# Convolution taps at fixed, spread places in VectorE's order; its mixing, the gate's stores and a weight split moved

## The chip, the cores and the metric

The kernel runs on one core of one Trainium2 chip. The metric is the device time of one execution in microseconds, the median of several runs. A profiled execution of the same kernel gives the trace.

## The reference

One layer over a sequence of 2048 tokens of 1024 features (float32). The input is normalised, projected once, and mixed in three ways: chunked attention (6 heads), a convolution of 31 taps over 256 channels, and retention (6 heads). The three outputs go through one output projection onto the residual; then come a feed-forward part and a gated embedding. What the change touches is the convolution and the gate at the end:

```python
def conformer_conv(u, conv_w, conv_b, ln_g, ln_b, pw_w, pw_b):
    a, gate = jnp.split(u, 2, axis=-1)
    glu = a * jax.nn.sigmoid(gate)
    y = lax.conv_general_dilated(glu, conv_w[:, None, :], window_strides=(1,),
        padding=[(CONV_K - 1, 0)], feature_group_count=D_CONV, ...)
    y = layernorm(y + conv_b, ln_g, ln_b)
    y = jax.nn.silu(y)
    return y @ pw_w + pw_b

h = h + jnp.concatenate([att, conv, ret], axis=-1) @ w_o[i]
h = h + jnp.square(jax.nn.relu(rmsnorm(h, norm_ffn_g[i]) @ w1[i])) @ w2[i]
gate = jax.nn.sigmoid(rmsnorm(h, norm_ple_g[i]) @ w_pg[i])
h = h + gate * (p[i] @ w_ple[i])
```

## The kernel before

The sequence is worked through in four blocks of 512 tokens (b = 0 to 3). Features lie on partitions, tokens along the free dimension. Each product is made of three matmuls, since every operand is split into a high and a low part (names ending in h and l, or two slices of a weight tile w); the low part of a weight is a subtraction `wsplit` (L125 to L127) on VectorE or GpSimd, after ScalarE has made the high part. A weight is loaded raw and split at its first use, stored to DRAM split (`wstage`, L129), and afterwards loaded split (`wunit`, L133, load at L139). Weight tiles have five buffers, raw loads two.

The stages of a block are: the convolution's projection (four chunks, `conv_proj`, L293); in blocks 1 to 3 then the gate of the block before (two halves of four columns, `gate`, L746); three pairs of an attention projection ap and a retention projection rp; the output projection (two parts); eight feed-forward groups. The gate of block 3 comes at the very end. For a column j of the gate TensorE makes 24 matmuls into a bank acc and 6 into a bank ple. VectorE reads acc (L768), ScalarE takes the sigmoid, VectorE multiplies with ple (L771), POOL adds to h (L772), and SP stores h to `out` (L773). Accumulators acc have two banks.

TensorE's instructions are pinned to their written order (`tc.keep_in_program_order`, L48 to L59): an instruction so pinned comes right behind the instruction of its engine that was written before it. All others are placed by a scheduler that goes by readiness and priority: `tc.high_priority(offset=...)` moves a priority, and LATE is the lowest one. Side work is woven into the written order by position: `place` names points along TensorE's work where the next step of a generator is written, `spread` gives evenly spaced points, and `chain` paces a generator between a start and an end point (L808 to L846). So attention's mixing (`att_mix`) is written among the matmuls of ap and rp: its scores are sc on TensorE, the biased scores with their row extreme pt on VectorE (L472), their transposes back in sc, copied to pT on VectorE (L486), and their product with v in po.

The convolution itself has two groups of 128 channels, and for each a first tap L338 and 30 more L340, all on VectorE with 128x512 elements: y = gl * weight + y. Before, the 62 taps of a block are written at the end of `conv_proj` at priority LATE. `conv_mix` (L352) takes y: transposes on TensorE to the bank cvt, a layer norm on VectorE and POOL (z), transposes back to the bank cvb, silu and split on ScalarE and VectorE, and the pointwise product into the bank cpw.

Of the kernel before, what the change touches and what calls it, by code (L numbers as in the profile page):

```python
# [14 lines left out]
ALU = mybir.AluOpType  # L15
AX = mybir.AxisListType

P = 128
D = 1024
S = 2048  # L20
T = 512
NB = S // T
# [5 lines left out]
NTAP = 31  # L28
# [6 lines left out]
LATE = -1000  # L35
# [5 lines left out]
def trunk(ctx, tc, a, out):  # L41
    nc = tc.nc
    V, A, G = nc.vector, nc.scalar, nc.gpsimd
# [29 lines left out]
    def stile(tag, bufs, shape, name=None, dt=F32):  # L73
        return sp.tile(list(shape), dt, tag=tag, name=name or tag, bufs=bufs)
# [16 lines left out]
    def tmp(name, n):  # L91
        return stile("t", 4, [P, n], name)
# [4 lines left out]
    def cv(name, dt=F32, n=T):  # L97
        return stile("cv", 5, [P, n], name, dt)
# [19 lines left out]
    def f(t):  # L118
        return t.bitcast(F32)


    def wtile():
        return stile("w", 5, [P, 2, 2, HALF], "w", F32R)

    def wsplit(w, x, n, eng):  # L125
        A.activation(w[:, 0, :n], x, AF.Copy)  # L126
        eng.tensor_tensor(w[:, 1, :n], x, f(w[:, 0, :n]), ALU.subtract)  # L127
# [5 lines left out]
    def wunit(name, i, n=HALF):  # L133
        key = name + "_".join(map(str, i))
        seen[key] = seen.get(key, 0) + 1
        with tc.high_priority(offset=AHEAD):
            u = wtile()
            if key in kept:
                nc.sync.dma_start(f(u)[:, :, :, :n], kept[key])  # L139
            else:  # L140
                raw = rawt("raw")
                nc.sync.dma_start(raw[:, : 2 * n], a[name][i])
                for c in range(2):
                    wsplit(u[:, c], raw[:, c * n : c * n + n], n, (G, V)[c])
        if key not in kept and seen[key] == (2 if name == "w2" else 1):
            wstage(key, u, n)
        return [u[:, 0], u[:, 1]]
# [11 lines left out]
    def cost(n):  # L159
        return 3 * n / 2400.0  # L160

    def stream(name, *i):
        got = {}

        def blk(n):
            if n // 8 not in got:
                got.clear()
                got[n // 8] = wunit(name, (*i, n // 8))
            return tuple(got[n // 8][n % 8 // 4][:, s, (n % 4) * P : (n % 4) * P + P] for s in range(2))

        return blk
# [88 lines left out]
    cur = {}  # L260
# [32 lines left out]
    def conv_proj(blk):  # L293
        xh, xl = cur["x"]
        hi, lo = (lambda k: xh[:, k]), (lambda k: xl[:, k])
        gls = []

        def sigmoid(b):
            sig = tmp("sig", T)
            V.tensor_tensor(sig, b, cur["R"], ALU.mult)  # L300
            A.activation(sig, sig, AF.Sigmoid)
            G.tensor_tensor(sig, sig, cur["R"], ALU.mult)
            return sig

        def glu(c, b, sig):
            gl = cv("gl", n=T + NTAP - 1)
            V.tensor_copy(gl[:, : NTAP - 1], hist[:, c])
            V.tensor_tensor(gl[:, NTAP - 1 :], b, sig, ALU.mult)
            V.tensor_copy(hist[:, c], gl[:, T:])
            gls.append(gl)  # L310

        if blk == 0:
            ss = [sb2("cvp") for _ in range(2)]
            bs = [s[:, i * 512 : i * 512 + 512] for s in ss for i in range(2)]
            for i in range(4):
                if i == 3:
                    cur["R"] = cv("R")
                    bcast(cur["r"], cur["R"])
                yield from stat_steps(cur["w"][i], KT, hi, lo, bs[i], T)
            for c in range(2):  # L320
                glu(c, bs[2 * c + 1], sigmoid(bs[2 * c]))
        else:
            for c in range(2):
                if c == 0:
                    cur["R"] = cv("R")
                    bcast(cur["r"], cur["R"])
                b = accb()
                yield from stat_steps(wstat("wc", 2 * c), KT, hi, lo, b, T)
                sig = sigmoid(b)
                b = accb()  # L330
                yield from stat_steps(wstat("wc", 2 * c + 1), KT, hi, lo, b, T)
                glu(c, b, sig)
        ys = []
        with tc.high_priority(offset=LATE):
            for c in range(2):
                gl = gls[c]
                y = cv("y")
                V.tensor_scalar(y, gl[:, :T], cw[:, c, 0:1], cvec[:, 0, c : c + 1], ALU.mult, ALU.add)  # L338
                for j in range(1, NTAP):
                    V.scalar_tensor_tensor(y, gl[:, j : j + T], cw[:, c, j : j + 1], y, ALU.mult, ALU.add)  # L340
                ys.append(y)
        cur["ys"] = ys

    def load_pw():
        cur["pw"] = pww = ctile("pww", [P, 2, 2 * DC], dt=F32R)
# [400 lines left out]
    def gate(blk, half):  # L746
        xh, xl = cur["x3"]
        h = cur["h"]
        tk = slice(blk * T, blk * T + T)
        pt = cur["pt"]  # L750
        w = stream("w_g", half)
        for i in range(4):
            j = 4 * half + i
            end = blk == NB - 1 and j == KT - 1
            ws = [w(10 * i + k) for k in range(10)]
            for x in (slice(0, T // 2), slice(T // 2, T)) if end else (slice(0, T),):
                n = x.stop - x.start
                gt = tmp("gate", T)[:, :n]
                o = None
                for k in (*range(2), *range(2, 10)) if j == 0 else (*range(2, 10), *range(2)):  # L760
                    if k == 0:
                        o = e = sb2("ple")[:, :n]
                    elif k == 2:
                        o = b = accb()[:, :n]
                    y = pt[k] if k < 2 else (xh[:, k - 2], xl[:, k - 2])
                    yield from mm3s(o, ws[k], (y[0][:, x], y[1][:, x]), k in (0, 2), k in (1, 9))
                    if k == 9:
                        V.tensor_tensor(gt, b, cur["r3"][:, x], ALU.mult)  # L768
                        A.activation(gt, gt, AF.Sigmoid)
                    if k == (9 if j == 0 else 1):  # L770
                        V.tensor_tensor(gt, gt, e, ALU.mult)  # L771
                        (V if end else G).tensor_tensor(h[j][:, x], h[j][:, x], gt, ALU.add)  # L772
                        nc.sync.dma_start(out[j * P : j * P + P, blk * T + x.start : blk * T + x.stop], h[j][:, x])  # L773
                    yield cost(n) / 3

    kvc = [(None, None)] * NPAIR
    ng_ = DFF // 512
# [28 lines left out]
    AS, RS, RT0, CS, CE, RE, LE, LF, NE, NF, GE, GF, AS0, CS0, CE0 = 0.25, 0.35, 0.03, 0.4, 0.5, 0.95, 0.4, 0.7, 0.4, 0.55, 0.16, 0.22, 0.25, 0.5, 0.5  # L806

    def at(name, frac):  # L808
        s, c = start[name]
        return s + frac * c  # L810

    def spread(n, t0, t1):
        return [t0 + (t1 - t0) * i / (n - 1) for i in range(n)]

    def place(gen, ts):
        tasks.append([ts, gen, None])
# [3 lines left out]
    def chain(i, gen, start, end):  # L820
        chains[i].append([start, end, gen, None, 0.0])

    L = NB - 1
    place(load_pw, [at(("ap", 0, 0), 0.5)])
    for b in range(NB):
        if b:
            place(lambda b=b: xnorm(b), spread(13, at(("g2", b - 1, 6), 0.05), at(("g2", b - 1, 7), 0.95)))
            place(late, spread(8, at(("conv", b), 0.01), at(("conv", b), LE)))
            place(lambda b=b: ple_load(b - 1), [at(("conv", b), 0.3)])
            place(late_rstd, [at(("conv", b), LF), at(("conv", b), LF + 0.28)])  # L830
        if b:
            chain(1, conv_mix, at(("ap", b, 0), CS), at(("ap", b, 1), CE))
        for p in range(NPAIR):
            nxt = ("rp", b, p + 1) if p < 2 else ("wob", b)
            chain(0, lambda p=p: att_mix(p), at(("rp", b, p), AS if b or p else AS0), at(nxt, AS if p < 2 else 0.0))
            chain(1, lambda p=p: ret_mix(p), at(("ap", b, p + 1), RS) if p < 2 else at(("woa", b), RT0),
                  at(nxt, RE if p < 2 else 0.0))
            if b == 0 and p == 0:
                chain(1, conv_mix, at(("ap", b, 1), CS0), at(("rp", b, 2), CE0))
        place(norm2, [at(("g1", b, 0), NE), at(("g1", b, 0), NF)])  # L840
    place(lambda: ple_load(L), [at(("g2", L, 7), 0.0)])
    place(late_rstd, [at(("gate", L, 0), GE), at(("gate", L, 0), GF)])

# [35 lines left out]
    raw = rawt("raw")  # L879
    u = wtile()  # L880
    with tc.high_priority(offset=3 * AHEAD):
        nc.sync.dma_start(ng, a["norm_g"])
    for c in range(2):
        with tc.high_priority(offset=AHEAD):
            next(first)
        x = slice(c * HALF, c * HALF + HALF)
# [16 lines left out]
    cw = ctile("cw", [P, 2, NTAP], a["conv_w"])  # L903
    cvec = ctile("cvec", [P, 4, 2], a["cvec"])
# [114 lines left out]
```

## Time and profile before

| | us |
|---|---|
| median of 3 runs (lowest, highest) | 2763.8 (2763.01, 2765.96) |
| the profiled execution | 2768.22 |
| its span, first to last instruction | 2766.4 |
| TensorE busy in it | 2683.5 (97%) |
| VectorE busy | 1344.3 (49%) |
| ScalarE busy | 745.3 (27%) |
| GpSimd busy | 717.6 (26%) |

The mean granted clock of TensorE over the span is 0.99 of full speed. The names of the engines in rows are PE (TensorE; PEld its weight loads), DVE (VectorE), ACT (ScalarE), POOL (GpSimd) and SP (SyncE, which issues the DMAs; SPq is its sequencer). A busy share is an average over stages of different limits: of TensorE's idle time, what counts is which wait ended last, and on what.

### The profile page before, as it was taken

The numbers are of one execution on the slowest core, as the hardware profiler recorded it, in microseconds if no ns is written. First come the engines' busy times: TensorE is split into PE (matmuls) and PEld (weight loads), VectorE is DVE, ScalarE is ACT, GpSimd is POOL, SyncE is SP. The second block draws the span as 40 slices with busy tenths as digits, with TensorE's granted clock in tenths as the row PEclk, the third lists the DMA queues.
The fourth block names the chain that finished last, engine by engine and source line by source line (L and its number), as shares of the span: only waits on it lengthen the run. The fifth ranks groups of instructions, "written<-read, shape, count | busy, mean of one in ns | idle before, by whom it ended". The sixth has DMA issues, their size and how long they took to land.

```text
span 2766.4 us, 34253 instructions
## 1 busy us (share of the span) xinstructions
PE 2683.5 (97%) x13178; PEld 2236.1 (81%) x13178; DVE 1344.3 (49%) x2297; ACT 745.3 (27%) x1506; POOL 717.6 (26%) x676
## 2 busy tenths in 40 slices
PE   7899999999899999999999999999999999999999
PEld 6777788887788888888888888888887888888887
DVE  5966655457745543334664554222376555322222
ACT  4454322234144321112324432000122442100011
POOL 4334534334312231222322213001022221210112
PEclk9999999999999999999999999999999999999999
DMA  7647664656633566767663345555655344555554
GB/s 270 237 146 259 230 215 170 208 176 219 206 121 128 193 212 231 259 222 261 240 208 116 132 156 210 187 194 195 231 191 178 117 151 160 190 192 189 197 195 147
DMA packets 123281, 535.35 MB, mean 194 GB/s; under 512 B 12784, under 2 KB 38128, under 8 KB 77040
## 3 DMA queue, kind: packets, MB, share of 16 engines
q1 hardware_dynamic: 123120, 533.17, 54.7%
q8 instruction: 104, 1.70, 0.3%
q14 instruction: 57, 0.47, 0.1%
HBM read 412.54 MB, written 120.59 MB: 193 GB/s over the span
## 4 chain that ended last, share of the span: by engine, by line
PE 82%; DVE 8%; DMA 4%; ACT 2%; issue 2%; POOL 1%; SPq 0%; DVEq 0%; ACTq 0%; POOLq 0%
PE acc L54 46%; PE w L54 26%; DVE y L340 4%; PE po L54 2%; PE sc L54 2%; PE sc L59 2%; DMA w<-k_wr 1%; PE rout L54 1%; DVE w L127 1%; PE ple L54 1%; PE rsc L54 1%; DMA w<-k_wa 1%; DVE k L445 1%; ACT q L447 0%; DMA raw<-in_wc_dram 0%
## 5 line engine op out<-in xcount | busy, mean ns | idle before, releaser
L54 PE MATMUL acc<-xh,w 128*128 128x512 f32 (+1 forms) x1744 | 549.1, 391 | 8.3 <-DVE gate L768 4.0
L54 PE MATMUL acc<-w,xh 128*128 128x512 f32 (+1 forms) x1536 | 469.0, 380 | 18.0 <-DMA w<-k_wa 6.7
L54 PEld LDWEIGHTS acc<-xh,w 128*128 128x128 f32 x1744 | 327.0, 188 | 80.0 <-issue 5.2
L54 PE MATMUL acc<-hid,w 128*128 128x512 f32 x1536 | 367.0, 392 | 0.0
L54 PE MATMUL w<-hid,w 128*128 128x512 f32 x1536 | 362.0, 391 | 0.0
L54 PEld LDWEIGHTS acc<-hid,w 128*128 128x128 f32 x1536 | 288.4, 188 | 63.6
L54 PEld LDWEIGHTS w<-hid,w 128*128 128x128 f32 x1536 | 288.5, 188 | 63.1
L54 PEld LDWEIGHTS acc<-w,xh 128*128 128x128 f32 x1536 | 287.8, 194 | 61.1 <-DMA w<-k_wr 9.5
L54 PE MATMUL acc<-xl,w 128*128 128x512 f32 (+1 forms) x872 | 335.0, 389 | 0.9 <-DVE xl L234 0.9
L54 PE MATMUL w<-xh,w 128*128 128x512 f32 x1024 | 322.0, 390 | 0.0
L127 POOL TENSOR_TENSOR w<-raw,w 128x512 fp32r<-128x512 f32 (+1 forms) x141 | 186.7, 1325 | 506.3 <-ACT w L126 486.6
L692 POOL TENSOR_TENSOR s<-r 128x512 f32<-128x512 f32 x128 | 157.7, 1233 | 554.9 <-DVE r L691 554.9
L126 ACT ACTIVATE w<-raw 128x512 fp32r<-128x512 f32 (+1 forms) x284 | 160.9, 614 | 498.1 <-PE acc L54 279.6
L54 PE MATMUL acc<-w,xl 128*128 128x384 f32 (+1 forms) x768 | 289.2, 377 | 0.0
L693 ACT ACTIVATE hid<-r 128x512 fp32r<-128x512 f32 x128 | 80.2, 628 | 576.3 <-DVE r L691 576.3
L54 PEld LDWEIGHTS w<-xh,w 128*128 128x128 f32 x1024 | 191.9, 188 | 39.7
L127 DVE TENSOR_TENSOR w<-raw,w 128x512 fp32r<-128x512 f32 (+1 forms) x143 | 180.5, 1263 | 81.9 <-ACT w L126 76.7
L340 DVE SCALAR_TENSOR_TENSOR y<-gl,cw,y 128x512 f32<-128x512 f32 x240 | 207.4, 893 | 2.5
L54 PE MATMUL w<-xl,w 128*128 128x512 f32 x512 | 199.2, 389 | 0.0
L54 PEld LDWEIGHTS acc<-xl,w 128*128 128x128 f32 x872 | 164.2, 188 | 36.1 <-DVE xl L234 1.3
L718 DVE TENSOR_TENSOR h<-h,w 128x512 f32<-128x512 f32 x128 | 87.9, 688 | 197.4 <-PE w L54 196.6
L718 DVE TENSOR_TENSOR h<-h,acc 128x512 f32<-128x512 f32 x128 | 87.8, 687 | 173.3 <-PE acc L54 172.8
(182 smaller groups left out, 3291.2 us busy)
## 6 DMA issues: line engine op xcount, KB each, us to landing
w<-k_w SPq DMA_DIRECT2D x160, 1024.0 KB, 4.8
k_w<-w SPq DMA_DIRECT2D x64, 1024.0 KB, 6.8
raw<-in_w_dram SPq DMA_DIRECT2D x96, 512.0 KB, 4.5
w<-k_wr SPq DMA_DIRECT2D x36, 1024.0 KB, 5.9
w<-k_w_g SPq DMA_DIRECT2D x30, 1024.0 KB, 4.8
w<-k_wa SPq DMA_DIRECT2D x36, 768.0 KB, 6.0
w<-k_w_oa SPq DMA_DIRECT2D x18, 1024.0 KB, 6.1
k_wr<-w SPq DMA_DIRECT2D x12, 1024.0 KB, 7.0
```

Of the source, the lines that this page charges most:

```text
L54: tc.keep_in_program_order(nc.tensor.matmul(o, x, y, start=start, stop=stop))
L59: tc.keep_in_program_order(nc.tensor.transpose(o, x, i))
L126: A.activation(w[:, 0, :n], x, AF.Copy)
L127: eng.tensor_tensor(w[:, 1, :n], x, f(w[:, 0, :n]), ALU.subtract)
L340: V.scalar_tensor_tensor(y, gl[:, j : j + T], cw[:, c, j : j + 1], y, ALU.mult, ALU.add)
L445: V.scalar_tensor_tensor(lo, bj, gain[x, 0:1], f(hi), ALU.mult, ALU.subtract)
L692: G.tensor_tensor(s, r, r, ALU.mult)
L693: A.activation(hid[:, j], r, AF.Square)
L718: V.tensor_tensor(h[j], h[j], b, ALU.add)
```

## The change

It has four parts.

- The taps leave `conv_proj` and become a generator `taps`. Each tap is pinned in VectorE's order behind the instruction written before it, and the 62 are written at evenly spaced points: in block 0 from 0.05 of ap of the first pair to 0.45 of ap of the second; in blocks 1 to 3 from 0.02 of the gate's first half to 0.8 of ap of the first pair.
- In blocks 1 to 3 `conv_mix` is written from 0.9 of the first ap to 0.95 of the first rp, instead of from 0.4 of the first ap to 0.5 of the second ap.
- In `gate` a store is held and issued at k == 6 of the next column, pinned in SP's order; the last of a half is issued at its end.
- The gate's weights w_g are split on GpSimd in both halves (before: one half on GpSimd, one on VectorE). They are split in block 1 only, 10 units, so 10 instructions of 128x512 change engine.

```diff
-                    wsplit(u[:, c], raw[:, c * n : c * n + n], n, (G, V)[c])
+                    wsplit(u[:, c], raw[:, c * n : c * n + n], n, G if name == "w_g" else (G, V)[c])
...
-        ys = []
-        with tc.high_priority(offset=LATE):
-            for c in range(2):
-                gl = gls[c]
-                y = cv("y")
-                V.tensor_scalar(y, gl[:, :T], cw[:, c, 0:1], cvec[:, 0, c : c + 1], ALU.mult, ALU.add)
-                for j in range(1, NTAP):
-                    V.scalar_tensor_tensor(y, gl[:, j : j + T], cw[:, c, j : j + 1], y, ALU.mult, ALU.add)
-                ys.append(y)
-        cur["ys"] = ys
+        cur["gls"] = gls
+
+    def taps():
+        ys = cur["ys"] = []
+        for c in range(2):
+            gl = cur["gls"][c]
+            y = cv("y")
+            ys.append(y)
+            for j in range(NTAP):
+                x, g = gl[:, j : j + T], cw[:, c, j : j + 1]
+                if j == 0:
+                    i = V.tensor_scalar(y, x, g, cvec[:, 0, c : c + 1], ALU.mult, ALU.add)
+                else:
+                    i = V.scalar_tensor_tensor(y, x, g, y, ALU.mult, ALU.add)
+                tc.keep_in_program_order(i)
+                yield
...
-                        nc.sync.dma_start(out[j * P : j * P + P, blk * T + x.start : blk * T + x.stop], h[j][:, x])
+                        held.append((out[j * P : j * P + P, blk * T + x.start : blk * T + x.stop], h[j][:, x]))
+                    if held and (end or k == 6):
+                        tc.keep_in_program_order(nc.sync.dma_start(*held.pop()))
                     yield cost(n) / 3
+
+        while held:
+            tc.keep_in_program_order(nc.sync.dma_start(*held.pop()))
...
+    for b in range(NB):
+        if b:
+            place(taps, spread(2 * NTAP, at(("gate", b - 1, 0), 0.02), at(("ap", b, 0), 0.8)))
+        else:
+            place(taps, spread(2 * NTAP, at(("ap", 0, 0), 0.05), at(("ap", 0, 1), 0.45)))
...
-            chain(1, conv_mix, at(("ap", b, 0), CS), at(("ap", b, 1), CE))
+            chain(1, conv_mix, at(("ap", b, 0), 0.9), at(("rp", b, 0), 0.95))
```

What the change moves in the order of the engines is shown at three places. "xN" means that a row stands N times in a row; lines are those of the version itself (in the changed one the taps are L344 and L346).

The first is VectorE in block 0, from the keys k of the first pair of heads to the score reductions (ISA pt,nm) of its first tile. Before:

```order
L445 SCALAR_TENSOR_TENSOR k<-qkT,kg,k 64x512
L566 RECIPROCAL e<-e 128x128
L445 SCALAR_TENSOR_TENSOR k<-qkT,kg,k 64x512
L472 ISA pt,nm<-sc,bias 128x128
L472 ISA nm 128x1
L340 SCALAR_TENSOR_TENSOR y<-gl,cw,y 128x512
L472 ISA pt,nm<-sc,bias 128x128
L472 ISA nm 128x1
```

And in the changed kernel, from the first reduction on:

```order
L478 ISA pt,nm<-sc,bias 128x128
L478 ISA nm 128x1
L346 SCALAR_TENSOR_TENSOR y<-gl,cw,y 128x512
L451 SCALAR_TENSOR_TENSOR k<-qkT,kg,k 64x512
L346 SCALAR_TENSOR_TENSOR y<-gl,cw,y 128x512
L571 TENSOR_SCALAR e<-e 128x128
L346 SCALAR_TENSOR_TENSOR y<-gl,cw,y 128x512
L572 RECIPROCAL e<-e 128x128
L346 SCALAR_TENSOR_TENSOR y<-gl,cw,y 128x512
L344 TENSOR_SCALAR y<-gl,cw,cvec 128x512
L346 SCALAR_TENSOR_TENSOR y<-gl,cw,y 128x512 x13
L478 ISA pt,nm<-sc,bias 128x128
```

Between the second k and the second reduction stand 17 taps, where none stood between the two and one between the reductions. Ahead of the second k stand 13 taps, where 28 stood.

The second is VectorE in block 1, around the gate's first columns (gate<-acc, L768 and in the changed kernel L775). Before, behind the second gl:

```order
L308 TENSOR_TENSOR gl<-acc,sig 128x512
L340 SCALAR_TENSOR_TENSOR y<-gl,cw,y 128x512
L127 TENSOR_TENSOR w<-raw,w 128x512
L309 COPY hist<-gl 128x30
L340 SCALAR_TENSOR_TENSOR y<-gl,cw,y 128x512
L338 TENSOR_SCALAR y<-gl,cw,cvec 128x512
L340 SCALAR_TENSOR_TENSOR y<-gl,cw,y 128x512 x5
L127 TENSOR_TENSOR w<-raw,w 128x512
L768 TENSOR_TENSOR gate<-acc,r_5326 128x512
L340 SCALAR_TENSOR_TENSOR y<-gl,cw,y 128x512 x2
L771 TENSOR_TENSOR gate<-gate,ple 128x512
L340 SCALAR_TENSOR_TENSOR y<-gl,cw,y 128x512 x4
```

In the changed kernel, behind the second gl as well:

```order
L308 TENSOR_TENSOR gl<-acc,sig 128x512
L309 COPY hist<-gl 128x30
L344 TENSOR_SCALAR y<-gl,cw,cvec 128x512
L346 SCALAR_TENSOR_TENSOR y<-gl,cw,y 128x512 x5
L775 TENSOR_TENSOR gate<-acc,r_5326 128x512
L778 TENSOR_TENSOR gate<-gate,ple 128x512
L346 SCALAR_TENSOR_TENSOR y<-gl,cw,y 128x512 x5
L775 TENSOR_TENSOR gate<-acc,r_5326 128x512
L346 SCALAR_TENSOR_TENSOR y<-gl,cw,y 128x512
L778 TENSOR_TENSOR gate<-gate,ple 128x512
```

The taps of the first channel group no longer stand ahead of the second gl, and the splits w are gone from VectorE. So it goes on, with six taps or so to each column; 13 taps are left behind the last column.

The third is SP in block 1: the last stores of the gate (out_dram) and the loads of the attention weights (w<-k_wa) among them. Before:

```order
L139 DMA w<-k_wa_0_414 128x4x384
L773 DMA out_dram<-h 128x512
L131 DMA k_w_g_4_5798<-w 128x2048
L139 DMA w<-k_wa_1_423 128x4x384
L773 DMA out_dram<-h 128x512
L139 DMA w<-k_wa_2_432 128x4x384
L773 DMA out_dram<-h 128x512
L139 DMA w<-k_wa_3_441 128x4x384
```

In the changed kernel:

```order
L139 DMA w<-k_wa_0_350 128x4x384
L782 DMA out_dram<-h 128x512
L131 DMA k_w_g_4_5778<-w 128x2048
L139 DMA w<-k_wa_1_359 128x4x384
L782 DMA out_dram<-h 128x512
L139 DMA w<-k_wa_2_368 128x4x384
L782 DMA out_dram<-h 128x512
L139 DMA w<-k_wa_3_377 128x4x384
```

The rows are the same; in both, four stores stand ahead of the first of these loads.

## Rows read from the trace of the kernel before

**Rows 1.** The page: busy time by engine, the chain by engine, the taps' group.

```profile
PE 2683.5 (97%) x13178; PEld 2236.1 (81%) x13178; DVE 1344.3 (49%) x2297; ACT 745.3 (27%) x1506; POOL 717.6 (26%) x676
...
PE 82%; DVE 8%; DMA 4%; ACT 2%; issue 2%; POOL 1%; SPq 0%; DVEq 0%; ACTq 0%; POOLq 0%
...
L340 DVE SCALAR_TENSOR_TENSOR y<-gl,cw,y 128x512 f32<-128x512 f32 x240 | 207.4, 893 | 2.5
```

**Rows 2.** TensorE's waits: us in total, times, longest us.

```profile
PE sc L54 <- DVE k L445: 21.6, 22, 2.6
PE qkT L59 <- POOL an L416: 10.2, 4, 6.6
...
PE acc L54 <- DMA w<-k_wa: 6.7, 3, 5.3
...
PE acc L54 <- DVE gate L768: 4.2, 4, 1.6
...
PE acc L54 <- DVE gl L308: 2.3, 1, 2.3
```

**Rows 3.** Windows: length, busy PE, PEld, DVE, ACT, POOL (count), clock, DMA.

```profile
80.00:120.00 40.00, 37.15 (x205) 31.96 (x206) 37.71 (x81) 17.54 (x52) 12.97 (x14) 0.94 0.62 226
...
695.00:735.00 40.00, 35.99 (x154) 28.54 (x154) 39.56 (x48) 6.30 (x11) 14.48 (x10) 1.00 0.72 251
```

**Rows 4.** VectorE's timeline in block 0: start us, us, instruction, idle before.

```profile
79.15 0.75 DVE L445 SCALAR_TENSOR_TENSOR k<-qkT,kg,k 64x512 fp32r<-64x512 f32 x1
...
80.81 0.28 DVE L472 CUSTOM_DVE_ANT_0 pt<-sc,bias 128x128 f32<-128x128 f32 x1
...
134.48 4.97 DVE L340 SCALAR_TENSOR_TENSOR y<-gl,cw,y 128x512 f32<-128x512 f32 x5
```

**Rows 5.** Timelines of VectorE and POOL: taps beside POOL's splits, taps alone.

```profile
58.38 2.77 DVE L340 SCALAR_TENSOR_TENSOR y<-gl,cw,y 128x512 f32<-128x512 f32 x2
...
58.90 3.39 POOL L127 TENSOR_TENSOR w<-raw,w 128x512 fp32r<-128x512 f32 x2
...
686.74 3.38 DVE L340 SCALAR_TENSOR_TENSOR y<-gl,cw,y 128x512 f32<-128x512 f32 x5
```

**Rows 6.** TensorE's timeline in block 0, scores and keys.

```profile
87.09 0.38 PE L59 MATMUL sc<-ident,pt 128*128 128x128 f32 x2
...
94.87 0.66 PE L59 MATMUL sc<-ident,pt 128*128 128x128 f32 x4
...
99.40 0.44 PE L54 MATMUL sc<-k,q 128*128 128x384 f32 x1 [1.44 <-DVE pT L486]
...
141.06 1.33 PE L59 MATMUL qkT<-ident,an 128*128 128x128 f32 x5 [6.59 <-POOL an L416]
...
154.63 0.63 PE L59 MATMUL cvt<-ident,y 128*128 128x128 f32 x4 [2.35 <-DVE z L371]
```

**Rows 7.** TensorE's timeline in block 1; the last row is of the chain.

```profile
681.76 0.39 PE L54 MATMUL acc<-xh,w 128*128 128x512 f32 x1
...
739.58 0.62 PE L54 MATMUL acc<-w,xh 128*128 128x384 f32 x2 [0.17 <-DVE gate L768]
...
748.78 1.01 PE L54 MATMUL acc<-w,xh 128*128 128x384 f32 x2 [5.28 <-DMA w<-k_wa]
...
1010.20 10.88 PE acc L54 x48
```

**Rows 8.** Timelines of VectorE, POOL and SP: column 6 of the gate.

```profile
738.85 0.68 DVE L768 TENSOR_TENSOR gate<-acc,r 128x512 f32<-128x512 f32 x1
...
740.99 1.30 POOL L772 TENSOR_TENSOR h<-h,gate 128x512 f32<-128x512 f32 x1 [5.77 <-DVE gate L771]
...
742.78 0.53 SPq L139 DMA_DIRECT2D w<-k_wa  x1
```

**Rows 9.** Timelines of VectorE and TensorE in block 2, last gate and transposes.

```profile
1423.55 0.69 DVE L771 TENSOR_TENSOR gate<-gate,ple 128x512 f32<-128x512 f32 x1 [0.71 <-ACT gate L769]
...
1431.09 0.60 PE L59 MATMUL cvt<-ident,y 128*128 128x128 f32 x4
```

More of the change, by code (lines that the diff above doesn't have):

```diff
@@ L751, in gate @@
         w = stream("w_g", half)
+        held = []
         for i in range(4):
```

## Prediction

> **What bounds the kernel now.** I read the page's busy shares and chain first, then TensorE's waits, the windows, and at the end the timelines of the two stretches where the change moves rows. TensorE is busy 2683.5 us of the 2766.4 us span, and by the chain 82% of the span is TensorE's and 8% VectorE's [rows 1]. So all that can be won is TensorE's idle time of some 83 us and the slow clock behind each stall, and only where a stall stands. The waits show which ones end on VectorE or on something behind it [rows 2]: sc on k 21.6 us, qkT on POOL's an 10.2, acc on the gate 4.2, acc on gl 2.3, and acc on the load of k_wa 6.7. The feed-forward stretches have none of these and no tap, so they stay as they are. The windows [rows 3] show where VectorE is short: busy 37.71 of 40 us in block 0's scores, and 39.56 in the gate that block 1 does for block 0.
>
> **Block 0: taps in a worse place.** Before, a tap was VectorE's last choice and filled idle time: 28 of 62 taps stood ahead of the second k (L445) [rows 4]. Now each tap is pinned behind its neighbour. The order has 13 ahead of that k, and 17 between it and the second score reduction, where one stood. A tap alone takes 0.67 us (3.38 for five) [rows 5]. The 15 that no longer fill the wait for weights and keys cost 15 x 0.67 = 10.0 us later, in the stretch with 37.71 of 40 us taken.
> Going down the new order by the old durations: the second k ends near 78.1 (79.90 before; it waits for fewer taps). Then 17 x 0.67 = 11.4, and 1.1 for an e and a reciprocal: the reduction, at 80.81 before [rows 4], starts near 90.6. TensorE's transposes of the first tile's pt, at 87.09 before [rows 6], start near 91.3 (+4). From 91.0, ten taps (6.7) and 2.6 us of rotary rows and a split lead to the copy pT at 100.3. Six more taps and the same other rows lead to the second tile's reductions near 108, its transposes near 110.4 (94.87 before, +15.5) and the third tile's second scores near 117.3 (99.40 before, +17.9).
> By then nearly all taps are done, while before 17 were still to come: 17 x 0.67 = 11.4 us lighter. That is where TensorE waited 6.59 us for qkT and 2.35 for cvt [rows 6]. I take these two, 8.9 us, as won back: **+9**. Bounds: +6.5 if the whole 11.4 come back, +17.9 if nothing does. I take a value near the low end, because right before the longer of these waits ended VectorE had five taps in a row, 4.97 us [rows 4].
>
> **Block 1: gates less late.** After the last product of the first gate bank (681.76) seven more banks of 30 matmuls at 0.227 us (10.88 for 48) [rows 7] take 47.6 us, so attention could start near 729.7. It started at 739.58, after 2.3 us of waits on gl, 4.2 on gates [rows 2] and slower matmuls behind them. Then came 5.28 us for k_wa [rows 7]: SP issued this load at 742.78, behind the store of column 6 of the gate, which waits for POOL's add at 740.99, and this for VectorE's gate row at 738.85 [rows 8]. So what counts is when VectorE reaches column 6.
> In the new order both gl stand ahead of all taps, 42 taps stand ahead of this gate row where 62 did, and the ten splits of w_g are POOL's. The first tap can start near 676 (second gl, whose bank TensorE finishes a little before). 42 x 0.667 = 28.0, and six pairs of gate rows at 1.3 make 7.8. POOL's work takes time from VectorE: two taps beside two of POOL's splits took 2.77 us instead of 1.4 [rows 5], and the mean tap is 893 ns [rows 1]. I take 1.05 us for each POOL instruction of 128x512 that falls on a tap; twelve splits and six adds do: 18.9. Sum 730.7 against 738.85: **-8.1**, and k_wa lands as much earlier. The ends of that price: at nothing VectorE reaches column 6 at 711.8, ahead of TensorE (724.3), the load is issued near 728 and lands near 734, where it is wanted at 733.6: -14.7. At 1.44 us a piece the gate comes at 737.7: -1. By the same sum the banks of columns 4 to 6 are read 6 to 8 us late, just inside the 8.2 us (36 matmuls) that two banks allow.
> The rows show that a tap beside POOL is stretched by about its own length. The Trainium skill, in "SBUF — State Buffer", section "Who interferes with whom", is stricter: a VectorE instruction with two inputs in SBUF and a GpSimd instruction that reads SBUF share a port pair, which the first one holds for its whole instruction while the other is blocked. By that rule a tap may wait POOL's whole 1.30 us [rows 8], 23.4 us for the 18, and block 1 would gain 3.6 only. The trace shows less, some 1.05, and the sum goes by that.
>
> **Later stores.** A store is held until k = 6 of the next column, but on SP each load of k_wa keeps the number of stores ahead of it: four, five, six and seven. The last still stands right behind the store of column 6. I cost this at 0: SP, the only queue these are on, waits at that place for POOL in any case. POOL's add of column 3 now stands behind five splits and may be some 5 us later; nothing in VectorE's order waits for it before column 7.
>
> **The mixing later, blocks 1 to 3.** The same matmuls, transposes and ScalarE rows, moved. The transposes of y stand 48 matmuls of 128x384 further on (8.3 us at 0.173), and cvb follows qkT at once, so that silu and yh stand on ScalarE between the rows that make k. In blocks 2 and 3 the waits for k_wa (6.7 in three, of which 5.28 are block 1's) may go, while sc's waits on k grow by 0.3 to 0.5: -0.5 a block, **-1** together. Thirteen taps now stand between the last gate row and the transposes. From 1424.2 [rows 9] they (8.7), two pairs of ass rows and the waits for these end near 1438.6; the transposes, at 1431.09 before, are due near 1439.4. The cover is under a microsecond; behind it TensorE waits at once: up to +2 a block.
>
> **Sum.** +9 - 8.1 - 1 = about 0. The profiled execution took 2768.2 us, 4.4 over the median of 2763.8, so the changed kernel's median comes out at **2763.5 us**.
>
> **Rivals.**
> - *Gates freed wholly.* Taps and POOL's splits collide less, since they take turns in an order of their own: block 1 gives 14.7, block 0 its low 6.5, the rest 1: -9, 2754.6. For it: in blocks 2 and 3, without splits, TensorE waits for no gate (the four waits on gates are block 1's). Against it: 893 ns as the mean tap.
> - *Block 0 not won back (slower).* The queue on VectorE up to the third tile's scores costs 17.9, and the wait for qkT is no shorter, because its own chain (an, on POOL behind the retention's norm) starts later by as much. 17.9 - 8.1 - 1 = +8.8, 2772.6. It is decided at the second part of the second pair's qkT: if a stall of over 5 us stands there still, this is it. For it: that wait ends on POOL, not on VectorE. Against it: the five taps just before.
> - *POOL eats block 1.* At 1.44 us a collision -1 instead of -8.1: +7, 2770.8.
> - *The change doesn't do in block 0 what its order says.* The queue is absorbed by waits that TensorE has there anyway, such as sc on k (longest 2.6): block 0 at 0 to +2, so -8, 2755.8. Against it: the delays above are worked out behind these waits.
>
> **Chances.** The forecast 0.42, gates freed 0.19, block 0 not won back 0.19, POOL 0.10, absorbed 0.10. A measurement of this kernel can tell about 0.2%, 5.5 us, from no change. Faster by more: 0.19 + 0.10 = 0.29; slower by more: 0.19 + 0.10 = 0.29; within: 0.42. The range, 2754.0 to 2773.0, takes in the forecast with its bounds and the centres of the rivals, and leaves out what lies beyond these; the forecast's own range is 2758.5 to 2769.
>
> **What would show it.** Right: seventeen taps in a row of work ahead of the second score reduction, TensorE's first transposes near 91, the third tile's scores some 18 us later than before, and the qkT stall behind them at most 2 us; in block 1 no wait on gl, the gate row of column 6 some 8 us nearer to the stretch's start than before, and k_wa's wait still there. Wrong: a shift at the start of block 0's feed-forward under 6 or over 13 us, or waits of acc on w in block 1's gate, where POOL would then deliver weights too late.

## The result and the profile after

The changed kernel takes 2780.64 us (median of 4 runs, 2777.69 to 2783.29) against 2763.81: a ratio of 1.0059, 95% interval 1.0042 to 1.0077, slower by some 17 us. The forecast was 2763.5 with a range to 2773.0. The profiled execution took 2783.29 us, its span is 2781.5, 15.1 longer than before, at a mean clock of 0.985. On the page of the changed kernel, busy times by engine and the chain by engine:

```profile
PE 2693.5 (97%) x13178; PEld 2247.6 (81%) x13178; DVE 1344.2 (48%) x2287; ACT 744.2 (27%) x1506; POOL 736.5 (26%) x686
...
PE 85%; DVE 5%; DMA 3%; ACT 3%; issue 2%; POOL 1%; SPq 0%; DVEq 0%; ACTq 0%; POOLq 0%
```

VectorE's share of the chain fell from 8% to 5%, and the kernel is slower all the same. TensorE's waits (us in total, times, longest) answer to [rows 2]:

```profile
PE sc L54 <- DVE k L451: 14.3, 14, 2.6
PE sc L54 <- DVE pT L492: 9.3, 2, 5.7
PE qkT L59 <- POOL an L422: 8.1, 5, 2.4
PE acc L54 <- ACT rn L560: 7.9, 4, 2.7
PE sc L59 <- ACT pt L480: 7.6, 2, 5.0
...
PE acc L54 <- DVE gate L775: 3.8, 3, 1.7
PE cvt L59 <- DVE z L377: 3.8, 1, 3.8
PE ms L54 <- POOL sq L240: 2.3, 1, 2.3
...
PE acc L54 <- DMA w<-k_wa: 1.5, 2, 0.8
```

The waits on gl, on k_wa (6.7 before) and on the longest an (6.6) went or shrank. In their place stand waits on pT and pt, both of block 0's scores, on rn, and on sq. Where the time went is seen from the start of each block's first matmul that reads hid, the inner values of the feed-forward part (acc<-hid), here as the shift against the kernel before. Such a matmul comes at 344.49, 1037.24, 1719.11 and 2398.86 us before, and at 358.19, 1050.88, 1731.51 and 2413.93 after. So block 0 lost 13.7 us, block 1 gave 0.1, block 2 gave 1.2 and block 3 lost 2.7.

**Block 0.** Timelines of VectorE and then of TensorE in the changed kernel; they answer to [rows 4, 6]:

```profile
75.67 0.76 DVE L451 SCALAR_TENSOR_TENSOR k<-qkT,kg,k 64x512 fp32r<-64x512 f32 x1
...
79.97 8.69 DVE L346 SCALAR_TENSOR_TENSOR y<-gl,cw,y 128x512 f32<-128x512 f32 x13
88.68 0.29 DVE L478 CUSTOM_DVE_ANT_0 pt<-sc,bias 128x128 f32<-128x128 f32 x1
...
99.12 0.28 DVE L492 COPY pT<-sc 128x128 f32<-128x128 f32 x1
```

```profile
89.56 0.47 PE L59 MATMUL sc<-ident,pt 128*128 128x128 f32 x1 [5.05 <-ACT pt L480]
...
99.46 0.58 PE L54 MATMUL sc<-k,q 128*128 128x256 f32 x1 [5.75 <-DVE pT L492]
...
109.08 0.93 PE L59 MATMUL sc<-ident,pt 128*128 128x128 f32 x4 [2.52 <-ACT pt L480]
...
117.56 0.69 PE L54 MATMUL sc<-k,q 128*128 128x384 f32 x1 [3.55 <-DVE pT L492]
...
155.34 0.76 PE L59 MATMUL qkT<-ident,an 128*128 128x128 f32 x5 [1.53 <-POOL an L422]
...
167.15 0.63 PE L59 MATMUL cvt<-ident,y 128*128 128x128 f32 x4 [3.79 <-DVE z L377]
```

The thirteen taps in a row hold the second reduction until 88.68; TensorE then waits four times for what stands behind taps on VectorE.

**Block 1.** TensorE reached the gate's norm sums ms, and there a wait is new. Timelines of VectorE, POOL, ScalarE and TensorE in the changed kernel (take 13.7 off to compare with before):

```profile
665.76 9.54 DVE L234 SCALAR_TENSOR_TENSOR xl<-h,ng,xh 128x512 fp32r<-128x512 f32 x8
...
666.00 3.36 POOL L127 TENSOR_TENSOR w<-raw,w 128x512 fp32r<-128x512 f32 x2 [5.68 <-ACT w L126]
671.76 2.99 POOL L127 TENSOR_TENSOR w<-raw,w 128x512 fp32r<-128x512 f32 x2 [2.40 <-ACT w L126]
...
675.94 0.63 ACT L301 ACTIVATE sig<-sig 128x512 f32<-128x512 f32 x1 [2.43 <-DVE sig L300]
676.47 0.62 ACT L239 ACTIVATE q<-h 128x512 f32<-128x512 f32 x1
...
681.97 1.27 POOL L240 TENSOR_TENSOR sq<-sq,q 128x512 f32<-128x512 f32 x1 [0.74 <-ACT q L239]
...
683.29 1.83 PE L54 MATMUL ms<-ones,sq 128*128 128x1 f32 x8 [2.31 <-POOL sq L240]
...
695.44 1.65 DVE L344 TENSOR_SCALAR y<-gl,cw,cvec 128x512 f32<-128x512 f32 x1
...
750.92 0.68 DVE L775 TENSOR_TENSOR gate<-acc,r 128x512 f32<-128x512 f32 x1
...
758.35 0.94 PE L54 MATMUL acc<-w,xh 128*128 128x384 f32 x2 [1.68 <-DVE gate L775]
```

And the same place before:

```profile
654.44 5.76 DVE L234 SCALAR_TENSOR_TENSOR xl<-h,ng,xh 128x512 fp32r<-128x512 f32 x7
...
658.41 0.61 ACT L239 ACTIVATE q<-h 128x512 f32<-128x512 f32 x1
...
660.83 0.63 ACT L301 ACTIVATE sig<-sig 128x512 f32<-128x512 f32 x1 [0.51 <-DVE sig L300]
...
665.57 1.48 POOL L240 TENSOR_TENSOR sq<-sq,q 128x512 f32<-128x512 f32 x1
...
667.12 1.03 PE L54 MATMUL ms<-ones,sq 128*128 128x1 f32 x8
```

Before, the last square ended at 667.05 and ms came at 667.12: there was no slack. After, four splits on POOL instead of two fall on VectorE's rows, its eight xl take 9.54 us (0.75 and 5.76 before), and the first of the last three squares on ScalarE (q) stands behind the sigmoid and not ahead of it:

```
before: L239 q<-h  L301 TABLE_LOAD  L301 sig<-sig  L239 q<-h  L741 ph<-praw x2  L239 q<-h
after:  L301 TABLE_LOAD  L301 sig<-sig  L239 q<-h x3
```

So q moves from 658.41 to 676.47 - 13.7 = 662.8, the last square ends 2.5 us late, and behind TensorE's wait its clock is low (0.69 over 11 us, shown at e5). The gate's first matmul of ple came at 674.99 before, and comes at 694.35: a shift of 19.4, 5.7 more than block 0 leaves. From that matmul VectorE reached column 6 after 750.92 - 694.35 = 56.6 us, against 738.85 - 674.99 = 63.9 [rows 8]. But all taps stand behind the second gl here, and the first one starts only at 695.44, that is 681.7 without block 0's shift. Without that shift column 6 comes at 737.2, 1.6 us earlier than before. The row of column 7, the last, follows 6.7 us later (757.62), since six taps stand between the two; before it followed 2.0 later (740.83). TensorE, already at attention's products, waits 1.68 us for that bank.

### The profile page after: what moved, and what is told of

It is laid out like the page before. It is cut to its first block, busy times and chain, and to the rows that moved or that the text cites. A ratio compares the mean times of both kernels' runs of the same rounds, so it can differ in the third digit from the quotient of the medians.

```text
span 2781.5 us, 34245 instructions
## 1 busy us (share of the span) xinstructions
PE 2693.5 (97%) x13178; PEld 2247.6 (81%) x13178; DVE 1344.2 (48%) x2287; ACT 744.2 (27%) x1506; POOL 736.5 (26%) x686
## 4 chain that ended last, share of the span: by engine, by line
PE 85%; DVE 5%; DMA 3%; ACT 3%; issue 2%; POOL 1%; SPq 0%; DVEq 0%; ACTq 0%; POOLq 0%
PE acc L54 49%; PE w L54 26%; PE sc L54 2%; PE po L54 2%; PE sc L59 2%; DVE y L346 2%; DMA w<-k_wr 2%; PE ple L54 1%; PE rout L54 1%; PE rsc L54 1%; DMA k_wc<-w 1%; DVE w L127 1%; DVE xl L234 1%; ACT q L453 1%; ACT w L126 0%
## 5 line engine op out<-in xcount | busy, mean ns | idle before, releaser
L54 PE MATMUL acc<-w,xh 128*128 128x512 f32 (+1 forms) x1536 | 474.6, 384 | 19.8 <-ACT rn L560 7.9
L54 PEld LDWEIGHTS acc<-w,xh 128*128 128x128 f32 x1536 | 293.7, 197 | 62.8 <-ACT rn L560 9.9
L127 POOL TENSOR_TENSOR w<-raw,w 128x512 fp32r<-128x512 f32 (+1 forms) x151 | 201.0, 1334 | 511.6 <-ACT w L126 476.6
L346 DVE SCALAR_TENSOR_TENSOR y<-gl,cw,y 128x512 f32<-128x512 f32 x240 | 214.6, 899 | 5.0
L127 DVE TENSOR_TENSOR w<-raw,w 128x512 fp32r<-128x512 f32 (+1 forms) x133 | 169.1, 1272 | 90.4 <-ACT w L126 86.3
```

The source lines that it names most:

```text
L54: tc.keep_in_program_order(nc.tensor.matmul(o, x, y, start=start, stop=stop))
L346: i = V.scalar_tensor_tensor(y, x, g, y, ALU.mult, ALU.add)
```

## The experiments

Each kernel is timed beside the kernel before on one chip. The blocks' columns are the change of each block's length in its profiled trace against the trace before, from the starts named above. The same code gave block 0 changes from -3.0 to +0.4 (e1, e6, e8 and e10 to e12), so differences of under 3 us of a single block are not read.

| kernel | median | ratio, 95% interval | block 0 | 1 | 2 | 3 |
|---|---|---|---|---|---|---|
| changed | 2780.6 | 1.0059 (1.0042 to 1.0077) | +13.7 | -0.1 | -1.2 | +2.7 |
| e5, changed again | 2776.7 | 1.0050 (1.0034 to 1.0066) | +12.3 | +0.3 | -1.5 | -1.7 |
| e1, block 0's taps old | 2763.6 | 0.9993 (0.9983 to 1.0002) | -0.7 | +0.1 | -5.0 | -1.2 |
| e2, w_g's split old | 2768.1 | 1.0007 (0.9997 to 1.0016) | +13.0 | -10.8 | +0.5 | -0.6 |
| e3, mixing old | 2787.5 | 1.0079 (1.0062 to 1.0095) | +12.8 | +3.8 | +3.7 | +3.0 |
| e4, stores old | 2777.4 | 1.0044 (1.0029 to 1.0059) | +15.3 | -1.2 | -4.6 | -1.3 |
| e6, e1 and e2 | 2752.8 | 0.9963 (0.9949 to 0.9977) | -3.0 | -11.2 | -2.4 | +0.1 |
| e7, block 0 not pinned | 2771.2 | 1.0024 (1.0013 to 1.0034) | +3.6 | +1.3 | -3.2 | +2.7 |
| e8, before, w_g on GpSimd | 2768.2 | 1.0016 (1.0007 to 1.0025) | -0.8 | +7.2 | -2.4 | -1.3 |
| e9, squares on VectorE | 2774.8 | 1.0038 (1.0023 to 1.0053) | +11.2 | -1.4 | -4.5 | -1.6 |
| e10, e6, taps early, mixing old | 2769.6 | 1.0015 (1.0004 to 1.0026) | -1.0 | -4.6 | +5.4 | +3.9 |
| e11, e6, taps early | 2763.8 | 0.9997 (0.9985 to 1.0008) | +0.4 | -5.6 | +0.5 | +2.4 |
| e12, e6, taps longer | 2761.1 | 0.9981 (0.9972 to 0.9991) | -2.6 | -7.6 | +2.0 | +2.4 |

**e1.** Block 0's taps go back into `conv_proj`, at LATE.

```diff
+        if blk == 0:
...
+            with tc.high_priority(offset=LATE):
+                for c in range(2):
...
+                    for j in range(1, NTAP):
+                        V.scalar_tensor_tensor(y, gl[:, j : j + T], cw[:, c, j : j + 1], y, ALU.mult, ALU.add)
...
-            place(taps, spread(2 * NTAP, at(("ap", 0, 0), 0.05), at(("ap", 0, 1), 0.45)))
```

> The changed kernel, with block 0's taps as before (lowest priority, written in the projection), the rest as changed. Theory (block 0's pinned taps stand ahead of the score chain): the shift of 13.7 us at block 0's first feed-forward matmul goes to under 1, the rest of the trace moves as one piece, and the median comes to 2780.6 - 13.7 = 2767, still some 3 over the kernel before. Rival (the later blocks lose what block 0 gives back, because they start with their queues further ahead): over 2772.

Block 0's loss is gone, and the median is 17 us lower (13 lower than that of e5). The theory holds; the rest of the change then gives nothing that can be told from no change.

**e2.** The split of w_g as before.

```diff
-                    wsplit(..., n, G if name == "w_g" else (G, V)[c])
+                    wsplit(..., n, (G, V)[c])
```

> The changed kernel, with w_g split half on GpSimd and half on VectorE as before. Theory (POOL's splits delay the squares for the gate's norm): TensorE's wait of ms on POOL's sq (2.31 us) and the slow matmuls behind it go, the gate of block 1 starts 13.7 us later than before instead of 19.4, and the median falls by 4 to 6, to about 2775.5; the gates on VectorE come back later by some of that. Rival (the splits on POOL free VectorE for the gates more than they cost): the gate row of column 6 comes later on VectorE than in the changed kernel and the median is equal or higher.

The wait on sq is gone and the gate starts 13.0 us later than before, as block 0 leaves it. But the gain is twice what was expected, 12.5 us: the gate too is shorter, 55.7 us from its first matmul to attention's first against 58.1 in the changed kernel, and there is one wait for k_wa. TensorE's waits in 655 to 760 us of e2:

```profile
PE acc L54 <- DMA w<-k_wa: 1.8, 1, 1.8
PE acc L54 <- DVE gate L775: 0.4, 1, 0.4
```

The rival falls: VectorE reaches column 6 at 739.96, earlier than in the changed kernel (750.92). With the old split block 1 gains 10.8 us over the kernel before. But e2 moves more than the engine of ten splits. VectorE's timeline in e2, around the second gl:

```profile
677.33 1.58 DVE L344 TENSOR_SCALAR y<-gl,cw,cvec 128x512 f32<-128x512 f32 x1
...
694.21 0.68 DVE L308 TENSOR_TENSOR gl<-acc,sig 128x512 f32<-128x512 f32 x1
```

The taps start 18 us earlier than in the changed kernel, and eleven of them stand ahead of the second gl, where it has none. As I read the code, a pinned tap comes behind the VectorE instruction written before it: with the old split that is a split of w_g, which runs early; with the new one it is the copy behind the second gl. All kernels here with the old split and pinned taps in block 1 start them behind the first gl, all with the new one behind the second. Eleven taps alone take 11 x 0.67 = 7.4 us. No run separates them from the splits on POOL.

**e3.** The mixing of blocks 1 to 3 at its old points. There it is written ahead of the last taps, so it reads y with some taps of the second channel group still to come, and its time is that of a mixing that waits for fewer of them.

```diff
-            chain(1, conv_mix, at(("ap", b, 0), 0.9), at(("rp", b, 0), 0.95))
+            chain(1, conv_mix, at(("ap", b, 0), CS), at(("ap", b, 1), CE))
```

> The changed kernel, with the convolution's mixing of blocks 1 to 3 at its old points. Theory (the mixing's place trades one wait for another): the waits of acc on ACT's rn (2.7, 2.5, 2.5) go, those of sc on k (2.9, 2.3, 2.2) come back, the transposes wait for late taps by up to 3 a block; together -2 to +6. Rival (the later mixing costs by itself): the median falls by over 5, to under 2775.

TensorE's waits in e3:

```profile
PE sc L54 <- DVE k L451: 21.2, 21, 2.6
PE cvt L59 <- DVE y L346: 9.8, 6, 1.9
...
PE acc L54 <- ACT rn L560: 0.6, 3, 0.3
```

Rn's wait (7.9) went, k's came back (14.3 to 21.2), and 9.8 us of waits for taps came on top: slower by some 7, just over the -2 to +6 expected, though the intervals of the two ratios overlap. The trade is real, and the later mixing is what covers the later taps.

**e4.** The gate's stores issued at once, not pinned.

```diff
-                        held.append((out[...], h[j][:, x]))
-                    if held and (end or k == 6):
-                        tc.keep_in_program_order(nc.sync.dma_start(*held.pop()))
+                        nc.sync.dma_start(out[...], h[j][:, x])
...
```

> The changed kernel, with the gate's stores issued where they were. Theory (their order on SP against the loads of k_wa is the same): within 2 us of the changed kernel. Rival (the pinned stores block weight loads): faster by over 3 us.

1.0044 against 1.0059 and 1.0050 for the changed kernel: no difference that can be told. Held stores cost and give nothing that shows here.

**e5.** The changed kernel once more.

> The changed kernel once more, beside the next three on one chip. Block 0 comes out 12.8 to 15.3 us longer and block 1 within 2 us of the kernel before, as in the four traces that have these parts; blocks 2 and 3 differ from trace to trace by up to 5 us, as the granted clock falls at other places. Median 2777 to 2783.

Close to that: block 0's +12.3 and the median of 2776.7 lie just under the stated ranges. It shows something more: the wait on sq is the same 2.31 us, but the gate starts only 14.8 us later than before, not 19.4. Windows of 11 us from that wait on (length; busy PE, PEld, DVE, ACT, POOL; granted clock; DMA), in the first trace and in e5's:

```profile
683.00:694.00 11.00, 10.71 (x38) 8.88 (x39) 0.85 (x2) 2.64 (x5) 9.89 (x9) 0.69 0.53 159
```

```profile
681.00:692.00 11.00, 10.09 (x50) 8.48 (x51) 1.23 (x3) 4.89 (x10) 11.00 (x10) 1.00 0.46 159
```

The same wait was followed by a granted clock of 0.69 in one execution and 1.00 in the other, 38 against 50 matmuls in the same time (1.00 is the higher of the two levels, 2.4 GHz; 0.69 is a mean of it and the lower one, 1.2 GHz). So behind the same wait the gate starts 5.7 us late in the one and 2.5 in the other, beyond what block 0 leaves. Yet block 1 as a whole ends alike, -0.1 and +0.3. VectorE's first tap and TensorE's waits for gate rows in 655 to 780 us of e5:

```profile
694.04 0.54 DVE L344 TENSOR_SCALAR y<-gl,cw,cvec 128x512 f32<-128x512 f32 x1
```

```profile
PE acc L54 <- DVE gate L775: 6.6, 3, 2.7
```

Without block 0's shift the first tap starts at 694.04 - 12.32 = 681.7, as in the first trace. TensorE is earlier but VectorE isn't, and so TensorE waits 6.6 us for gate rows instead of 3.8.

**e6.** e1 and e2 together.

> The changed kernel with block 0's taps and the split of w_g as before; what stays are the spread taps and the later mixing of blocks 1 to 3 and the held stores. Theory (the two parts are apart from each other: 17.0 and 12.5 us of the changed kernel's median): 2780.6 - 29.5 = 2751, 13 under the kernel before; block 0 within 1 us of before and block 1 shorter by 9 to 11. Rival (the split only mends what block 0 had disturbed, so the two overlap): 2761 to 2764, no faster than with block 0's taps alone put back.

2752.8: faster than the kernel before by 0.4%, and the best of all here. The two parts add up; the rival falls. (Block 0's -3.0 is more than the 1 us expected.) TensorE's waits in 655 to 760 us of e6:

```profile
PE acc L54 <- DMA w<-k_wa: 2.4, 1, 2.4
...
PE acc L54 <- DVE gate L786: 0.4, 1, 0.4
```

**e7.** Block 0's taps at the same places, not pinned.

```diff
-                tc.keep_in_program_order(i)
+                if pin:
+                    tc.keep_in_program_order(i)
-            place(taps, spread(2 * NTAP, at(("ap", 0, 0), 0.05), at(("ap", 0, 1), 0.45)))
+            place(lambda: taps(False), spread(2 * NTAP, at(("ap", 0, 0), 0.05), at(("ap", 0, 1), 0.45)))
```

> The changed kernel, where block 0's taps are written at the same spread places but not pinned. Four taps then stand between the second k and the second score reduction instead of 17, 35 ahead of that k instead of 13. Theory (the pin makes the queue: a tap can't fill idle time ahead of its neighbour): block 0 within +5 us of the kernel before, median 2768 to 2773. Rival (the places, so close together, make it): block 0 still over 10 us longer, median as the changed kernel's.

Block 0 loses 3.6 us instead of 12 to 14: most of it was the pin, as the theory says. Without the pin, but also without LATE's low priority, taps still delay the copies pT: TensorE waits 10.3 us for them, 1.4 before. TensorE's waits in 60 to 170 us of e7:

```profile
PE sc L54 <- DVE pT L493: 10.3, 2, 6.0
PE acc L54 <- POOL w L127: 5.8, 1, 5.8
```

**e8.** The kernel before, with only w_g's split moved.

```diff
-                    wsplit(u[:, c], raw[:, c * n : c * n + n], n, (G, V)[c])
+                    wsplit(u[:, c], raw[:, c * n : c * n + n], n, G if name == "w_g" else (G, V)[c])
```

> The kernel before, with only w_g's split moved to GpSimd. In POOL's order three of the squares for the gate's norm again stand behind the sigmoid's product. Theory (that order alone makes the wait of ms): ms waits some 2 to 5 us on POOL's sq, the gate of block 1 starts 4 to 6 later, and the gates, for which VectorE has ten splits less, win back some 3: 0 to +6. Rival (with taps at the lowest priority VectorE's relief is worth more): faster by over 3 us.

Slower by 0.16%, and block 1 longer by 7.2: ms waits and the eight xl take 9.54 us as in the changed kernel, while the gate wins nothing (its shift is 5.2 at its start and 6.1 at its end). So the split costs by itself, with the taps at LATE and many of them ahead of the second gl. TensorE's waits in 655 to 760 us of e8, and VectorE's timeline:

```profile
PE acc L54 <- DVE gate L768: 6.4, 3, 4.1
PE ms L54 <- POOL sq L240: 3.1, 1, 3.1
```

```profile
651.23 9.54 DVE L234 SCALAR_TENSOR_TENSOR xl<-h,ng,xh 128x512 fp32r<-128x512 f32 x8
```

**e9.** The squares' sums for the gate's norm on VectorE.

```diff
-            G.tensor_tensor(sq, sq, q, ALU.add)
+            eng.tensor_tensor(sq, sq, q, ALU.add)
...
-            rms_split(j, 2, x, sq)
+            rms_split(j, 2, x, sq, V)
```

> The changed kernel, with the squares for the gate's norm (blocks 0 to 2) summed on VectorE, which has no taps there, instead of POOL; w_g is split on POOL as in the change. Theory (what w_g costs ahead of the gate is that these squares stand late in POOL's order): the wait of ms on sq (2.3 us) goes, block 1's gate starts no later than block 0's shift tells (13 to 15 us), and the median falls by 2 to 6, but not to the 2768.1 of the old split, since POOL's splits still slow the taps in the gate. Rival (the wait has another cause, such as the weights' raw loads): a wait of like size stands at ms or at the gate's first weights, and the median stays.

A miss for the theory as it stood. The median is somewhat lower, but the intervals of the ratios overlap. The wait did not go, it moved to VectorE, where the squares wait for ScalarE's q. VectorE's timeline in e9, and TensorE's waits in 650 to 830 us:

```profile
675.97 1.37 DVE L240 TENSOR_TENSOR sq<-sq,q 128x512 f32<-128x512 f32 x1 [2.38 <-ACT q L239]
```

```profile
PE ms L54 <- DVE sq L240: 3.2, 1, 3.2
```

So it was not POOL's order that made the squares late but what stands ahead of them: ScalarE's q behind a sigmoid that waits for VectorE. That reading rests on rows: in e1, e5 and e8 too the last three q stand behind the sigmoid and ms waits, in e2 and e6 one of them stands ahead and it doesn't. A kernel with q put ahead of the sigmoid wasn't tried.

**e10, e11, e12.** From e6, the taps of blocks 1 to 3 end at another point: at 0.35 of the first ap (e10, e11) or at 0.5 of the first rp (e12). The mixing is at its old points (e10), as in e6 (e11), or behind the taps (e12).

```diff
-            place(taps, spread(2 * NTAP, at(("gate", b - 1, 0), 0.02), at(("ap", b, 0), 0.8)))
+            place(taps, spread(2 * NTAP, at(("gate", b - 1, 0), 0.02), at(("ap", b, 0), 0.35)))
```

> The kernel with block 0's taps and w_g's split as before (2752.8 us), but with the taps of blocks 1 to 3 written up to 0.35 instead of 0.8 of the first ap, and with the mixing at its old points behind them. Theory (the mixing's place trades one wait for another): acc's waits on ACT's rn (2.7, 2.5, 2.5) go, sc's on k (2.9, 2.3, 2.2) come back, median 2750 to 2757. Rival (the gain in block 1 came from moving taps out of the gate, or from the later mixing): 2760 or more.

> The same with the taps up to 0.35 of the first ap, and the mixing at the changed, later points. Theory: what the taps' places give in block 1 is a short queue ahead of the gate rows, and 7 instead of 6 taps a column cost some 0.7 us of lateness a column that the two banks still take: within 3 us of 2752.8. Rival (six a column is at the edge): waits of acc on the gate of 1 to 2 us in columns 4 to 6 and 2756 to 2760.

> The kernel with block 0's taps and w_g's split as before (2752.8 us), the taps of blocks 1 to 3 written up to 0.5 of the first rp instead of 0.8 of the first ap (five a column in the gate instead of six, some ten among the keys and scores of the first pair), and the mixing behind them, from 0.6 of that rp to 0.9 of the second ap. Theory (the gate's margin is what counts; seven a column gave 2763.8): block 1's waits on the gate and on k_wa (2.4) go, acc's waits on ACT's rn go with the mixing, sc's waits on k come back: 2747 to 2754. Rival (taps among the scores make a queue as in block 0): waits of sc on pT or pt of over 2 us in blocks 1 to 3 and 2756 or more.

All three are slower than e6, and none comes out in the range of its theory. In e11 seven taps a column give 2763.8, 11 us more than six; block 1's trace has 5.6 of them. The expected 0.7 us a column were taken by the banks, but for waits under 0.8, up to column 6 and then cost 4.1 at once, at the bank of column 7. So the rival has the direction, but wait and time are beyond its numbers. TensorE's waits in 655 to 760 us of e11:

```profile
PE acc L54 <- DVE gate L786: 5.1, 3, 4.1
```

e10 against e11 is the mixing alone, with all taps written ahead of it: 5.7 us slower at its old points, by blocks 2 and 3, where the transposes wait for taps; the rival's time (2760 or more) holds. In e12 five a column clear the gate (no wait on it in block 1), but the taps then stand among the first pair's keys and scores, and the mixing's own chain waits: in 1330 to 1540 us of e12

```profile
PE sc L54 <- DVE k L462: 3.6, 4, 1.7
PE cvb L59 <- ACT y L396: 1.5, 1, 1.5
PE cvt L59 <- DVE y L357: 1.4, 1, 1.4
```

and the rival's time (2756 or more) holds, though its waits on pT or pt are not seen; those on k, y and z took their part.

## Why the prediction was wrong

**Block 0, +9 forecast, +13.7 and +12.3 measured.** The queue was worked out rightly: second reduction 90.6 forecast and 88.68 measured, pT 100.3 and 99.12, the second tile's transposes 110.4 and 109.08, the third tile's second scores 117.3 and 117.56. The step that failed is "I take these two, 8.9 us, as won back". The shift went on to 20.1 at the first pair's transposes rqT (128.45, 108.32 before), and 6.4 of it came back. The wait for qkT did shrink, 6.59 to 1.53. The one for cvt didn't, 2.35 before and 3.79 after: it ends on VectorE's z after POOL's step of the norm, not on taps, and where block 0 is left as it was it is anything from 2.0 (e6) to 3.8 (e11). That VectorE is lighter helps only a wait that ends on VectorE's queue. The rival that nothing is won back (17.9) was about as far off on the other side, and its sign, a stall of over 5 us at that qkT, was not seen. e1 (the loss gone) and e7 (3.6 us left) show that the pinned order is the cause of most of it.

**Block 1, -8.1 forecast, -0.1 and +0.3 measured.** This is the term that turned "no change" into a loss. From the first tap on the working held: 42 taps, twelve splits and six adds stood there, and VectorE took 55.5 us to column 6 (695.44 to 750.92), where the sum has 730.7 - 676 = 54.7. The step that failed is "The first tap can start near 676". Without block 0's shift it started at 681.7 in both traces of the changed kernel, and column 6 came 1.6 and 2.7 us nearer instead of 8.1. The sum took the second gl, ahead of the taps, to be as early as TensorE's bank, and counted POOL's splits from the first tap on only. Four splits ahead of it fall on VectorE's eight xl, at the very price that was used: eight at 0.67 and four times 1.05 make 9.6, and 9.54 was measured. That, and ScalarE's order, which the forecast did not read, made ms wait 2.3 us. In the first trace the clock fell behind this, and gl waited for TensorE's late bank. In e5 the clock stayed, and gl waited for the product of the sigmoid on POOL, behind two more splits (687.78 to 690.32). So by these two traces it isn't the clock that the block lost by.

A second step failed: "what counts is when VectorE reaches column 6". The waits for k_wa did shrink, from 5.28 to two of 0.65 and 0.80. But TensorE waited 0.55 and 1.59 us for the banks of columns 3 and 4, where the sum had every bank read just inside the 8.2 us that two banks allow, and 1.68 us for that of column 7, whose row stands behind six more taps (2.69, 1.58 and 2.36 in e5).

I took the ten splits off VectorE's list as a gain and did not ask who else is on the two engines ahead of the gate. e8 (7.2 us lost in block 1 with nothing else changed) shows that the move costs by itself, e2 (12.5 us back) what it is worth in the changed kernel, the later start of the taps included. How much of that is the squares, the collisions or the taps' start stays open. The rival "POOL eats block 1" had nearly the right sum, -1, by another path: its place was to be the gate's taps, at 1.44 us a collision.

**Collisions.** Eight xl beside four splits took 9.54 us, 4.1 more than the 5.4 of eight alone (8 x 0.67, an estimate from the taps' rows); I had weighed such collisions for the taps only. The Trainium skill, page "SBUF — State Buffer", section "Who interferes with whom", says that a VectorE instruction with two inputs in SBUF, as xl has, contends with GpSimd's reads of SBUF; on who stands against whom the trace agrees, and the section gives no time for such a row.

**Stores.** Cost at 0, and e4 shows no difference.

**Mixing, -1 forecast for blocks 2 and 3.** Measured +1.4 in the first trace and -3.2 in the second. Sc's waits on k did not grow by 0.3 to 0.5; in the first pair of blocks 1 to 3 they went (21.6 us in all before, 14.3 after), and waits of acc on ACT's rn of up to 2.7 took their place (7.9 in four): silu and its table load stand ahead of rn on ScalarE. These two about cancel. The margin of the transposes behind the last taps, under a microsecond by the sum, held (no wait of cvt on y), and e10 shows that without the later mixing it would not have.

## What to carry to other kernels

A pin that keeps a filler behind its neighbour takes from the engine the right to use idle time: count how many fillers stand ahead of the next instruction on the path, before and after, and what the engine does while it waits there. When work moves from one engine to another, price its collisions with everything that runs on both in its whole stretch, prefetch included, and look for the step that had no slack before (here a square that ended 0.07 us ahead of its matmul). A filler pinned behind another instruction moves with it: look where the first one starts. A chain made lighter wins back only waits that end on it: read what each wait ends on before you call it won back.

## What was not expected of the hardware

The same 2.31 us wait of TensorE, at the same place of the same kernel, was followed by a granted clock of 0.69 over 11 us in one execution and 1.00 in another. The gate's start differed by 3.2 us for it, and block 1 as a whole by 0.3, since VectorE's rows came no earlier: what a stall costs is a range, and it depends on which wait ends last behind it. Single blocks of the same code scatter by some 3 us from trace to trace; whether the clock makes that isn't shown. And fp32 rows on VectorE other than taps pay POOL's splits alike: eight xl took 9.54 us beside four splits, and 6.5 in two rows of the kernel before, where one split of POOL's fell on them.
